# Output projection of a conv block: one PSUM bank a pair, the condition in PSUM for the shift columns, more low parts on Pool

## The chip, the cores and the metric

The kernel runs on one core of a Trainium2 chip. The metric is the device time of one execution in microseconds (us); lower is better. Three runs of the kernel before gave 1113.10, 1115.33 and 1116.34 us, a median of 1115.33.

Engines are named as in the profile: PE (TensorE, matrix products), DVE (VectorE), ACT (ScalarE), POOL (GpSimd) and SP (SyncE, which issues nearly all loads here). SBUF is the large on-chip memory and PSUM the small one into which PE writes. Here PSUM holds eight banks of 512 fp32 values for each of 128 partitions.

## What is computed

One decoder layer with a convolution mixer, on 256 tokens of width 2048, all in fp32. The part of the reference that runs:

```
cond = silu(c)
mod = cond @ mod_w + mod_b
sh1, sc1, g1, sh2, sc2, g2 = split(mod, 6)
h = rms_norm(x, norm1_g) * (1 + sc1) + sh1
u = h @ w_in + b_in;  a, gt = split(u, 2);  u = a * sigmoid(gt)
u = causal_depthwise_conv(u, dw_w, 31 taps) + dw_b
u = silu(layer_norm(u, ln_g, ln_b))
y = u @ w_out + b_out
x = x + (1 + g1) * y
h = rms_norm(x, norm2_g) * (1 + sc2) + sh2
x = x + (1 + g2) * (square(relu(h @ mlp_w1)) @ mlp_w2)
```

The change lies in `u @ w_out`, the residual behind it, and the computation of `sh2`, which runs in the same stage.

## The kernel before

**Splitting.** A matrix product in fp32 is made of three products of rounded parts. Each weight block `w` of 128 x 2048 values (one megabyte) is split in two halves of 128 x 1024: the high part `hi` is a rounding copy on ACT (line 203), and the low part `lo = w - hi` is a subtraction (line 206) on DVE or, for the jobs that the list `POOLED` (line 59) names, on POOL. There are six buffers for halves of each kind. The input is split likewise into tiles `hl` (lines 212 to 217, eight tiles of 256 columns of K). For the output product `mm` then issues, for each of 16 steps over K, three matmuls of 256 tokens: high x high (L227), high weight x low input (L228), low weight x high input (L229).

**Jobs.** `jobs` is a list of 16 input pairs, 8 output pairs and the MLP's blocks. A job `("out", i)` is pair i of 128-column tiles of the output projection, i from 0 to 7: two weight blocks, 96 matmuls. Ahead of each job the program splits the weights of the next one (`splits`). Pair 0 runs with K as its outer loop, since its input is still being normalised; pairs 1 to 7 do the first tile of the pair, then the second. Each pair accumulates in a tile `p` of the pool name "mm", of which there are two, each of two banks (line 779); the two tiles of the pair lie in different banks.

**Behind a pair** (lines 897 to 922): ACT scales and shifts both tiles in PSUM (L905), DVE adds the residual (L906), ACT squares (L908), POOL adds the squares up (L910, L913), ACT applies the second norm's scale (L917) and the result is split for the MLP (L214 on ACT, L217 on DVE).

**Shift columns.** `sh2` is a matrix-vector product done on DVE: 16 column blocks of 128 x 2048 of `mod_w`, one megabyte each, are multiplied with the condition, which is held broadcast to all partitions as `cb` in SBUF, and summed along the row in the same instruction (line 381, `mod_col`). `LATE_OUT` (line 51) places 1, 2, 2, 3, 3, 3, 1 and 1 of them behind pairs 0 to 7. At the end of pair 7 the bias is added (L928) and the shift is copied to a tile `shz` (L929), which the first job of the MLP multiplies (L322).

**Loads.** All blocks come through five buffers named "raw" in one order on SP (lines 163 to 184): the two blocks of the next pair, then the columns of this one. A load starts when one of the five is free: a weight block frees its buffer after its four split instructions, a column after its product.

**Order.** The order of instructions on each engine is fixed when the program is built, by a scheduler with priorities (`urgent`) and hand-made dependencies (`tc.issue_after`). Each engine runs its own instructions in order. PSUM tiles: "mm" two tiles of two banks, "acc" two tiles of one bank (`ps_two`, line 420), "small" and "row" one bank each. Ahead of the output stage "acc" holds the results of the SiLU that makes `hl` (lines 871 to 883).

Of the kernel before, what the change touches and what calls it, by code (L numbers as in the profile page):

```python
# [8 lines left out]
F32 = mybir.dt.float32  # L9
F32R = mybir.dt.float32r  # L10
AF = mybir.ActivationFunctionType
ALU = mybir.AluOpType
PSUM = bass.MemoryType.PSUM

P = 128
T = 256
D = 2048
KT = D // P
# [16 lines left out]
SH1, SC1, G1, SH2, SC2, G2 = range(6)  # L35
# [20 lines left out]
K_OUTER = [("out", 0), ("up", 0, 1)]  # L56
SIDE = 14
SPLIT_LOADS = [("col", SC1 * KT + KT - 1), ("col", SH1 * KT + KT - 1), ("first", KT - 1)]
POOLED = [("out", 0), ("out", 1), ("out", 2), ("up", 0, 1), ("up", 0, 2)]
LATE_GATE = {("down", 0): [1, 2, 1, 2, 2, 2, 1, 1], ("down", 1): [1, 1, 1, 1, 0, 0, 0, 0]}  # L60


# [1 line left out]
def conv_block(ctx: ExitStack, tc: tile.TileContext, x, vec, dwq, c_row, mod_r, mod_c, w_first, w_in, w_out, w1, w2, out):  # L64
    nc = tc.nc
# [15 lines left out]
    def col(name, j=0, n=1):  # L81
        at = VEC[name] + j
        return v[:, at : at + n]
# [79 lines left out]
    def top_up():  # L163
        while todo and waiting[home(todo[0])] < room[home(todo[0])]:
            key = todo.pop(0)
            tag = home(key)
            waiting[tag] += 1
            if tag == "raw":
                raw[key] = wts.tile([P, KT, P], F32, name="raw", bufs=RAW)
            elif tag == "first":  # L170
                raw[key] = start_pool.tile([P, 2 * HELD, P], F32, name="first", bufs=FIRST)
            elif tag == "x":
                raw[key] = x_pool.tile([P, KT, T], F32, name="x1")
            else:
                raw[key] = v[:, soon:]
                with tc.issue_after(state["load"].ins):
                    state["load"] = nc.sync.dma_start(dwq_sb, dwq)
            with tc.issue_after(state["load"].ins) if "load" in state else ExitStack():
                if key in SPLIT_LOADS:
                    first_half = nc.sync.dma_start(raw[key][:, 0:HALF], source(key)[:, 0:HALF])  # L180
                    with tc.issue_after(first_half.ins):
                        state["load"] = nc.sync.dma_start(raw[key][:, HALF:], source(key)[:, HALF:])
                else:
                    state["load"] = nc.sync.dma_start(raw[key], source(key))
# [27 lines left out]
    def split_act(dst, src, on_act=True):  # L212
        if on_act:
            state["hi_end"] = nc.scalar.activation(dst[:, :, 0:T], src, AF.Copy).ins  # L214
        else:
            nc.vector.tensor_copy(dst[:, :, 0:T], src)
        state["lo_end"] = nc.vector.tensor_tensor(dst[:, :, T : 2 * T], src, dst[:, :, 0:T].bitcast(F32), op=ALU.subtract).ins  # L217
# [158 lines left out]
    def mod_col(at):  # L376
        w = take(("col", at)).rearrange("p k n -> p (k n)")
        which, k = divmod(at, KT)
        acc = modc[:, at : at + 1]
        with tc.issue_after(state["e_end"]) if "e_end" in state else ExitStack():  # L380
            nc.vector.scalar_tensor_tensor(w, w, 1.0, cb, op0=ALU.mult, op1=ALU.mult, accum_out=acc)  # L381
        if which in amps:
            return nc.vector.scalar_tensor_tensor(
                amps[which][:, k : k + 1], acc, col("modb", at), col("n1g", k), op0=ALU.add, op1=ALU.mult
            )
        elif which != SH2:
            return mod_bias(at, 1, acc)

    def mods(keys):
        for key in keys:  # L390
            if key[0] == "mod":
                mod_chunk(*key[1:])
            else:
                mod_col(key[1])
# [25 lines left out]
    def ps_two():  # L420
        return ps.tile([P, 2, T], F32, name="acc", bufs=2)
# [40 lines left out]
    def by_tokens(job):  # L462
        return job[0] == "down" or job[0] == "up" and job[1:] not in ((0, 0), (0, 1))
# [300 lines left out]
    for n, job in enumerate(jobs):  # L764
# [10 lines left out]
            for key in parts_early:  # L775
                split_w(key, nc.gpsimd)
        kind, i = job[0], job[-1]
        if not by_tokens(job):
            p = ps.tile([P, 2, 2 * T], F32, name="mm", bufs=2)
        if by_tokens(job) and i % 2 == 0:  # L780
            sums[kind, i // 2] = regions(job == ("down", QUARTERS - 1, HALF - 2))
# [26 lines left out]
        if kind == "in":  # L808
# [46 lines left out]
            nc.gpsimd.memset(shz, 0.0)  # L855
            shc = x_pool.tile([P, 2 * UNSCALED], F32, name="shc")
            gb = x_pool.tile([P, KT], F32, name="gb")
            top_up()
            with tc.issue_after(state["sum_end"].ins):
                mods(rows[1:-1])  # L860
# [36 lines left out]
        if kind == "out":  # L897
# [21 lines left out]
                )  # L919
            xa[i] = mp.tile([P, 2, 2 * T], F32R, name="u2", bufs=HALF)  # L920
            split_act(xa[i], a)
            mods(after[job])
            if i == HALF - 2:
                table(AF.Abs_reciprocal_sqrt, ss[:, 0, 0:1])
            if i == HALF - 1:
                mod_finish()
                cs = slice(SH2 * KT, SH2 * KT + KT)
                nc.vector.tensor_tensor(modc[:, cs], modc[:, cs], col("modb", SH2 * KT, KT), op=ALU.add)  # L928
                nc.scalar.activation(shz[:, :, 0], modc[:, SH2 * KT : SH2 * KT + KT], AF.Copy)  # L929
                sp = ps.tile([P, 512], F32, name="small", bufs=1)  # L930
                column_sum(sp[:, 0:T], [sqacc, ss[:, 0, :], ss[:, 1, :]])
                r2 = sp[:, 0:T]
                rms_factor(sp[:, 0:T], sp[:, T : 2 * T], r2)
# [112 lines left out]
```

## Time and profile before

The profile is of one execution of 1112.88 us, whose span from the first instruction to the last is 1110.9 us, at a mean granted TensorE clock of 0.996.

| what | value |
|---|---|
| median of three runs | 1115.33 us |
| profiled execution | 1112.88 us |
| its span | 1110.9 us |
| output stage (first matmul of pair 0 to the shift row, L322) | 302.1 to 409.5 us |
| stage's column products, L381 on DVE, 16 | 41.8 us busy |
| stage's low parts on DVE, L206, up to 440 us | 28, 40.1 us busy |

A row of a time line gives the start in us from the span's start, the length, the engine, the line, the operation with output and inputs and their shapes, a count, and in brackets how long the engine had been idle and what ended that. A row of the view by line or tile gives the shortest, median and longest duration in ns. Durations of PE overlap, so its pace is read from the distance of the starts.

### The profile page before, as it was taken

The numbers are of one execution on the slowest core, as the hardware profiler recorded it, in microseconds if no ns is written. First come the engines' busy times: TensorE is split into PE (matmuls) and PEld (weight loads), VectorE is DVE, ScalarE is ACT, GpSimd is POOL, SyncE is SP. The second block draws the span as 40 slices with busy tenths as digits, with TensorE's granted clock in tenths as the row PEclk, the third lists the DMA queues.
The fourth block names the chain that finished last, engine by engine and source line by source line (L and its number), as shares of the span: only waits on it lengthen the run. The fifth ranks groups of instructions, "written<-read, shape, count | busy, mean of one in ns | idle before, by whom it ended". The sixth has DMA issues, their size and how long they took to land.

```text
span 1110.9 us, 15369 instructions
## 1 busy us (share of the span) xinstructions
PE 1087.3 (98%) x6018; PEld 893.0 (80%) x6018; DVE 767.9 (69%) x1014; ACT 506.7 (46%) x675; POOL 176.6 (16%) x106
## 2 busy tenths in 40 slices
PE   6999999999999899999999999999999999999998
PEld 3888876667699888888888888888888888888887
DVE  5777789987499987675885566744656565565553
ACT  4111396754674478443444444333444334444431
POOL 0000176467574244000000000000000000000000
PEclk8999999999999999999999999999999999999999
DMA  9999989878579976897997889857888967788641
GB/s 384 420 422 421 416 325 359 344 294 352 218 302 354 375 295 243 265 273 230 381 401 259 227 243 287 305 157 260 248 240 234 246 205 228 217 243 250 209 142 38
DMA packets 142314, 314.22 MB, mean 283 GB/s; under 512 B 87585, under 2 KB 105505, under 8 KB 107297
## 3 DMA queue, kind: packets, MB, share of 16 engines
q1 hardware_dynamic: 142096, 313.11, 81.3%
q8 instruction: 47, 0.77, 0.3%
q14 instruction: 25, 0.20, 0.1%
q10 hardware_dynamic: 146, 0.13, 0.0%
HBM read 301.15 MB, written 12.07 MB: 282 GB/s over the span
## 4 chain that ended last, share of the span: by engine, by line
PE 80%; DMA 10%; DVE 5%; issue 2%; POOL 2%; ACT 1%; SPq 0%; DVEq 0%; POOLq 0%; ACTq 0%
PE mm L255 20%; PE mm L254 20%; PE mm L256 20%; DMA raw<-mod_c 8%; PE mm L231 6%; PE mm L232 3%; DVE raw L381 3%; PE row L307 2%; PE mm L723 2%; DMA raw<-w_out 1%; POOL lo L206 1%; DVE lo L206 1%; PE mm L228 1%; PE mm L229 1%; PE mm L227 1%
## 5 line engine op out<-in xcount | busy, mean ns | idle before, releaser
L203 ACT ACTIVATE hi<-raw 128x1024 fp32r<-128x1024 f32 x320 | 334.2, 1058 | 355.6 <-PE mm L256 301.0
L206 DVE TENSOR_TENSOR lo<-raw,hi 128x1024 fp32r<-128x1024 f32 x269 | 332.7, 1246 | 173.0 <-ACT hi L203 172.5
L255 PE MATMUL mm<-lo,u 128*128 128x512 f32 x496 | 193.1, 389 | 0.0
L254 PE MATMUL mm<-hi,u 128*128 128x512 f32 x496 | 193.0, 389 | 0.0
L256 PE MATMUL mm<-hi,u 128*128 128x512 f32 x496 | 192.9, 389 | 0.0
L256 PE MATMUL mm<-hi,hl 128*128 128x512 f32 x480 | 186.7, 389 | 0.0
L255 PE MATMUL mm<-lo,hl 128*128 128x512 f32 x480 | 186.7, 389 | 0.0
L254 PE MATMUL mm<-hi,hl 128*128 128x512 f32 x480 | 186.7, 389 | 0.0
L381 DVE SCALAR_TENSOR_TENSOR raw<-raw,cond 128x2048 f32<-128x2048 f32 x62 | 147.1, 2374 | 47.6 <-DMA raw<-mod_c 47.5
L206 POOL TENSOR_TENSOR lo<-raw,hi 128x1024 fp32r<-128x1024 f32 x51 | 130.7, 2591 | 205.1 <-ACT hi L203 205.1
L255 PEld LDWEIGHTS mm<-lo,u 128*128 128x128 f32 x496 | 93.1, 188 | 19.4 <-DVE lo L206 0.4
L256 PEld LDWEIGHTS mm<-hi,u 128*128 128x128 f32 x496 | 93.1, 188 | 19.4
L254 PEld LDWEIGHTS mm<-hi,u 128*128 128x128 f32 x496 | 93.1, 188 | 19.0
L256 PEld LDWEIGHTS mm<-hi,hl 128*128 128x128 f32 x480 | 90.1, 188 | 18.8
L254 PEld LDWEIGHTS mm<-hi,hl 128*128 128x128 f32 x480 | 90.1, 188 | 18.8
L255 PEld LDWEIGHTS mm<-lo,hl 128*128 128x128 f32 x480 | 90.1, 188 | 18.6
L615 DVE SCALAR_TENSOR_TENSOR acc<-u,v,acc 128x256 f32<-128x256 f32 x224 | 94.5, 488 | 1.9
L229 PE MATMUL mm<-hl,lo 128*128 128x256 f32 x288 | 81.8, 284 | 3.4 <-DVE lo L206 3.2
L227 PE MATMUL mm<-hl,hi 128*128 128x256 f32 x288 | 81.2, 284 | 3.6 <-ACT hi L203 2.2
L231 PE MATMUL mm<-hl,hi 128*128 128x512 f32 x224 | 81.9, 406 | 0.0
L228 PE MATMUL mm<-hl,hi 128*128 128x256 f32 x288 | 81.6, 284 | 0.2 <-DVE hl L217 0.2
L550 PE MATMUL mm<-two,first 128*128 128x256 f32 x256 | 60.6, 391 | 8.4 <-ACT two L581 8.4
(170 smaller groups left out, 1189.6 us busy)
## 6 DMA issues: line engine op xcount, KB each, us to landing
raw<-w SPq DMA_DIRECT2D x128, 1024.0 KB, 5.4
raw<-mod_c SPq DMA_DIRECT2D x62, 1024.0 KB, 9.2
raw<-mod_r SPq DMA_DIRECT2D x32, 1024.0 KB, 7.7
raw<-w_in SPq DMA_DIRECT2D x16, 1024.0 KB, 7.0
raw<-w_out SPq DMA_DIRECT2D x16, 1024.0 KB, 7.0
first<-w_first SPq DMA_DIRECT2D x15, 1024.0 KB, 17.1
flat<-two SPq DMA_DIRECT2D x30, 256.0 KB, 2.7
two<-flat SPq DMA_DIRECT2D x120, 64.0 KB, 4.2
```

The lines of the kernel that those rows point to most:

```text
L203: state["w_hi"] = nc.scalar.activation(hi, w[:, ks, :], AF.Copy).ins
L206: end = by.tensor_tensor(lo, w[:, ks, :], hi.bitcast(F32), op=ALU.subtract)
L227: nc.tensor.matmul(out_p, w, m[:, 0:T], start=begin, stop=False)
L228: nc.tensor.matmul(out_p, w, m[:, T : 2 * T], start=False, stop=False)
L229: state["mm_end"] = nc.tensor.matmul(out_p, lo[:, k % HALF, :], m[:, 0:T], start=False, stop=end)
L231: nc.tensor.matmul(p[:, c, :], hi[:, k % HALF, :], m, start=(k == 0), stop=(k == KT - 1))
L254: nc.tensor.matmul(p, p_hi, hi, start=begin, stop=False)
L255: nc.tensor.matmul(p, p_hi, lo, start=False, stop=False)
L256: nc.tensor.matmul(p, p_lo, hi, start=False, stop=end)
L381: nc.vector.scalar_tensor_tensor(w, w, 1.0, cb, op0=ALU.mult, op1=ALU.mult, accum_out=acc)
L550: step = nc.tensor.matmul(held[n][:, c, :], w[:, 2 * n + c, :], h, start=k == 0 and c == 0, stop=k == KT - 1, skip_group_check=True)
L615: nc.vector.scalar_tensor_tensor(out, s, w, acc, op0=ALU.mult, op1=ALU.add)
```

## The change

It does four things in the output stage.

- Pairs 1 to 7 accumulate both tiles in one bank, a tile of the "acc" pool; pair 0 keeps "mm".
- Behind pair 1 the condition is copied by ACT into both "mm" tiles, 1024 values in each. The column products behind pairs 1 to 5 (13 of the 16) are done as two instructions of 1024 values, with the condition read from PSUM and the two sums in `modc` and a new tile `rest2`; the hand-made dependency on `e_end` is left out there. Behind pair 6 the copies are given up, and the last two columns are done as before, as is the one behind pair 0.
- The low parts of pairs 3, 4 and 5 move from DVE to POOL (`POOLED`), 12 halves.
- The bias is added to `rest2`, and `rest2` to the shift, where one addition stood.

```
-POOLED = [("out", 0), ("out", 1), ("out", 2), ("up", 0, 1), ("up", 0, 2)]
+POOLED = [("out", i) for i in range(6)] + [("up", 0, 1), ("up", 0, 2)]
+IN_PSUM = range(1, 6)
...
         acc = modc[:, at : at + 1]
+        if which == SH2 and "cond" in state:
+            n = HALF * P
+            for half, total in zip(state["cond"], (acc, rest2[:, k : k + 1])):
+                nc.vector.scalar_tensor_tensor(w[:, 0:n], w[:, 0:n], 1.0, half, op0=ALU.mult, op1=ALU.mult, accum_out=total)
+                w = w[:, n:]
+            return
         with tc.issue_after(state["e_end"]) if "e_end" in state else ExitStack():
...
-        if not by_tokens(job):
+        if kind == "out" and i > 0:
+            p = ps_two()
+        elif not by_tokens(job):
             p = ps.tile([P, 2, 2 * T], F32, name="mm", bufs=2)
...
+            rest2 = x_pool.tile([P, KT], F32, name="rest2")
+            nc.gpsimd.memset(rest2, 0.0)
...
             split_act(xa[i], a)
+            if i == IN_PSUM[0]:
+                state["cond"] = []
+                for h in range(2):
+                    half = ps.tile([P, 2, 2 * T], F32, name="mm", bufs=2).rearrange("p a b -> p (a b)")
+                    nc.scalar.activation(half, cb[:, h * HALF * P : (h + 1) * HALF * P], AF.Copy)
+                    state["cond"].append(half)
+            if i == IN_PSUM[-1] + 1:
+                del state["cond"]
             mods(after[job])
...
-                nc.vector.tensor_tensor(modc[:, cs], modc[:, cs], col("modb", SH2 * KT, KT), op=ALU.add)
+                nc.vector.tensor_tensor(rest2, rest2, col("modb", SH2 * KT, KT), op=ALU.add)
+                nc.vector.tensor_tensor(modc[:, cs], modc[:, cs], rest2, op=ALU.add)
```

SP issues the same loads in the same order. On POOL the twelve new low parts stand between the sums of squares.

## The prediction

> **What bounds the kernel now.** I read the page first, then the busy time of the engines in four stretches of the output stage, then TensorE's own rows around each wait, and last the rows of the engines that it waits for.
>
> ```profile
> span 1110.9 us, 15369 instructions
> ...
> PE 1087.3 (98%) x6018; PEld 893.0 (80%) x6018; DVE 767.9 (69%) x1014; ACT 506.7 (46%) x675; POOL 176.6 (16%) x106
> ```
>
> PE is busy 98% of the span, so a change elsewhere is worth only what PE now loses in waits. The edit touches one stage, pairs 0 to 7 of the output product, which the windows show (after each engine's time, the instructions; then clock, DMA share, GB/s):
>
> ```profile
> core 0: us, PE busy (x) PEld busy (x) DVE busy (x) ACT busy (x) POOL busy (x), PEclk, DMA share, GB/s
> 302.00:326.80 24.80, 24.44 (x200) 24.06 (x201) 22.19 (x31) 18.79 (x31) 17.54 (x8) 1.00 0.86 346
> 326.80:361.90 35.10, 34.97 (x292) 34.76 (x291) 35.10 (x28) 18.67 (x28) 20.08 (x10) 1.00 0.87 329
> 361.90:402.80 40.90, 35.50 (x290) 34.69 (x289) 37.78 (x35) 24.15 (x35) 7.61 (x7) 1.00 0.95 364
> ```
>
> The stretches are pairs 0 and 1, 2 to 4, and 5 to 7. DVE is full from pair 2 on, POOL has room, and in pairs 5 to 7 PE is idle for some 5 us. PE's rows name each wait (start, length, and in brackets the idle time before it and what ended that):
>
> ```profile
> 335.69 0.28 PE L228 MATMUL mm<-hl,hi 128*128 128x256 f32 x1
> 336.11 0.39 PE L229 MATMUL mm<-hl,lo 128*128 128x256 f32 x1
> ...
> 361.89 0.28 PE L227 MATMUL mm<-hl,hi 128*128 128x256 f32 x1
> 362.01 0.28 PE L228 MATMUL mm<-hl,hi 128*128 128x256 f32 x1
> 363.06 0.39 PE L229 MATMUL mm<-hl,lo 128*128 128x256 f32 x1 [0.78 <-DVE lo L206]
> ...
> 374.43 0.28 PE L227 MATMUL mm<-hl,hi 128*128 128x256 f32 x1
> 374.55 0.28 PE L228 MATMUL mm<-hl,hi 128*128 128x256 f32 x1
> 376.52 0.39 PE L229 MATMUL mm<-hl,lo 128*128 128x256 f32 x1 [1.69 <-DVE lo L206]
> ...
> 387.78 0.28 PE L229 MATMUL mm<-hl,lo 128*128 128x256 f32 x1
> 390.23 0.38 PE L227 MATMUL mm<-hl,hi 128*128 128x256 f32 x1 [2.17 <-ACT hi L203]
> ...
> 391.49 0.38 PE L229 MATMUL mm<-hl,lo 128*128 128x256 f32 x1 [0.76 <-DVE lo L206]
> ...
> 409.48 0.75 PE L322 MATMUL row<-raw,shz 128*32 128x128 f32 x20
> ```
>
> Products start 0.12 us apart (361.89, 362.01), so a step's excess over 0.12 is the loss: 0.30 in pair 2, 0.93 in pair 5, 1.85 in pair 6, and 2.33 and 0.92 in pair 7: 6.3 us. Pair 5 lasts from 361.89 to 374.43, 12.54 us; without its wait a pair is 11.6, or 96 products at 0.121. Counting back from 361.89 over three pairs and 0.30, pair 1 ends at 326.8; forward from 390.23 by 11.6 and 0.92, pair 7 ends at 402.8.
>
> **Why the low parts are late.** DVE and POOL hold each other up:
>
> ```profile
> 314.23 21.82 POOL L206 TENSOR_TENSOR lo<-raw,hi 128x1024 fp32r<-128x1024 f32 x6 [7.26 <-ACT hi L203]
> 314.54 4.24 DVE L381 SCALAR_TENSOR_TENSOR raw<-raw,cond 128x2048 f32<-128x2048 f32 x1
> 323.14 0.68 DVE L906 TENSOR_TENSOR x<-mm,x 128x512 f32<-128x512 f32 x1
> ...
> L381 DVE SCALAR_TENSOR_TENSOR raw<-raw,cond x62: 2277/2290/4239, 13.0 to 703.7; 128x2048 f32<-128x2048 f32 x62
> L206 POOL TENSOR_TENSOR lo<-raw,hi x51: 2375/2407/4480, 134.5 to 430.3; 128x1024 fp32r<-128x1024 f32 x51
> L206 DVE TENSOR_TENSOR lo<-raw,hi x269: 1181/1224/3424, 133.5 to 1091.4; 128x1024 fp32r<-128x1024 f32 x135
> L367 DVE SCALAR_TENSOR_TENSOR raw<-raw,cond x4: 1218/1224/1227, 123.5 to 127.9; 128x1024 f32<-128x1024 f32 x4
> ```
>
> A column product takes 2.29 us at the median and 4.24 where POOL holds a low part; POOL's takes 2.41 at the median and 4.48 at most, 3.64 on average in the run of six. Each excess (1.95 and 2.07) is about the other's length less its head start, so one waits until the other is through. L906, with one operand in PSUM, keeps its 0.68 us inside the same run of POOL. The eight products of L876, likewise half in PSUM, do so too:
>
> ```profile
> 296.80 10.17 POOL L875 TENSOR_TENSOR two<-cv,mu 128x512 f32<-128x512 f32 x8 [2.59 <-ACT mu L867]
> 299.53 1.88 DVE L876 TENSOR_TENSOR two<-two,small 128x512 f32<-128x512 f32 x3
> ```
>
> They stand 0.6 us apart while POOL goes on at 1.27. The Trainium skill ("SBUF — State Buffer", Who interferes with whom) states the same as a rule: two inputs in SBUF go through a read port shared with GpSimd and exclude it, one input doesn't. By that rule the new column products would not exclude POOL, and the trace agrees for L906 and L876 (0.68 us beside POOL).
>
> No row here shows the very form that is new, a product with a running sum and one operand in PSUM; that it excludes POOL all the same is rival B.
>
> **The change, part by part.**
>
> 1. *Twelve low parts of pairs 3 to 5 leave DVE.* That is 12 x 1.22 = 14.6 us, from an engine that is full from pair 2 to the start of pair 7. They cost POOL 12 x 2.41 = 29 us.
>
> 2. *Thirteen columns in halves, the condition in PSUM.* Nearest row: 1.22 us for a 1024-wide half in SBUF, 2.45 a column against 2.29, so 13 x 0.16 = 2.1 us more on DVE. From below it is nothing more than L381's rate (2.29); from above, 0.07 us more a half if PSUM costs what it seems to in L615 (0.488 us for 256 elements, where L413 takes 0.426):
>
> ```profile
> L615 DVE SCALAR_TENSOR_TENSOR acc<-u,v,acc 128x256 f32<-128x256 f32 x224 | 94.5, 488 | 1.9
> L413 DVE SCALAR_TENSOR_TENSOR small<-small,two 128x256 f32<-128x256 f32 x2 | 0.9, 426 | 1.0 <-ACT two L409 1.0
> ```
>
> I take 1.22. DVE is relieved of over 12 us on balance, which covers either end.
>
> 3. *Does POOL hold the pace?* Its six first low parts begin at 314.2 as before. The column of pair 0 is still a plain one and blocks the second, so the third starts at 321.1; the other columns no longer block, and four parts at 2.35 end at 330.5 instead of 336.0. PE needs the last of them in pair 2 at about 337, so the 0.30 goes. The first sum of squares makes it 331.4. Then, up to the last part of pair 5, stand 12 low parts (28.2), five sums (4.5 at 0.9) and four blocks by the residual's low part L217 (2.8): 366.9. The first part of pair 5 is ready about four parts or sums earlier, at 359, and PE wants it at 363.6 (pair 1's end in part 5, and three pairs of 11.6). POOL has 4.6 us in hand: the 0.93 goes.
>
> 4. *Pair 6* keeps its low parts on DVE, which now has nothing to finish first but a column each: the 1.85 goes. *Pair 7* still waits. Its high parts stand on ACT behind the eviction of pair 6:
>
> ```profile
> 388.10 1.11 ACT L905 ACTIVATE mm<-mm,gb,modc 128x256 f32<-128x256 f32 x2 [7.70 <-PE mm L229]
> 389.13 1.99 ACT L203 ACTIVATE hi<-raw 128x1024 fp32r<-128x1024 f32 x2
> ```
>
> In the built order one eviction instead of two stands ahead of them, so about 0.55 of 2.33 goes, and the 0.92 for the low part stays: 2.7 of 3.25 are left.
>
> 5. *One bank a pair from the "acc" pool.* This is what is lost. Before, pair 1's sums lie in "mm", and the built order puts 33 of its products among pair 0's, where PE would otherwise wait for the normalised input (hl). Now pair 1 needs an "acc" bank, which that stage's own results hold until the end, and only 11 products of pair 1 stand ahead of pair 0's last, all after its 84th. So PE follows the input:
>
> ```profile
> 311.25 1.29 DVE L217 TENSOR_TENSOR hl<-acc,hl 128x512 fp32r<-128x512 f32 x2
> 313.93 0.69 DVE L217 TENSOR_TENSOR hl<-acc,hl 128x512 fp32r<-128x512 f32 x1
> 315.07 0.95 PE L354 MATMUL row<-v,rowsb 128*128 128x4 f32 x8
> ```
>
> Input pair 5's low part is ready at 311.95. Eleven more products bring 313.3, one more and the row fold (0.95) 314.4, 34 products the end of pair 0 at 318.5 (the last input, ready at 314.6, is in time), 85 more the end of pair 1: 328.8 instead of 326.8. Loss 2.0. The same in the other direction: no loss if PE were never behind the input, which 33 borrowed products contradict.
>
> 6. *Two copies of the condition on ACT*, about 1.05 us each as the high parts (two in 1.99 above). The second waits for pair 0's eviction and lies beside PE's pair 1. The first stands early in the input's chain. ACT waits there twice for DVE, 0.36 and 0.58:
>
> ```profile
> 305.24 2.37 ACT L880 ACTIVATE acc<-two,v 128x256 f32<-128x256 f32 x4 [0.36 <-DVE hl L217]
> 308.83 2.16 ACT L880 ACTIVATE acc<-two,v 128x256 f32<-128x256 f32 x4 [0.58 <-DVE hl L217]
> ```
>
> That hides 0.94 of 1.05. I take 0.1; the bounds are 0 and 1.05. Columns of pair 1 keep their weight buffers until the second copy, near 330 instead of 323 and 328, but the low parts free theirs sooner, so loads aren't later. SP's order does not change.
>
> 7. *The end of the stage.* From pair 7's end PE needs 6.7 us to L322, 0.2 of it waiting for the shift columns, which end sooner: 0.2 goes. Two sums for one at the end are 16 elements wide: nothing.
>
> **Sum.** +2.0 + 0.1 - 0.30 - 0.93 - 1.85 - 0.55 - 0.2 = -1.7 us. Behind the stage PE's rows show no wait that would swallow it. The profiled execution has a span of 1110.9 in a time of 1112.88 and goes to 1111.2. The median of the runs is 1115.33, 2.45 above it: 1113.6 us, 0.15% less. 0.3%, or 3.35 us, is about what a measurement of this kernel can tell from no change.
>
> **Rivals.**
>
> *B, slower: the halves exclude POOL after all.* Place: POOL's queue for pairs 3 to 5. Then the low parts and columns stand in one line: from 321.1, 16 parts (37.6), sums (5.4), ten columns (23.0) and four L217 (2.8) end at 390 instead of 367, where PE wants the last part at 372.3 (the fourth of four quarters of pair 5): 17 us late. Less the margin that the estimate may overstate, some 15 over the forecast: 1128. It decides once POOL is blocked over 4.6 us before pair 5, 0.3 us for each of the 16 halves of pairs 2 to 4's eight columns. For it: two SBUF operands do this in row L381, and POOL then has no room. Against it: L906 and L876.
>
> *C, faster: pair 7's wait goes too.* If its high parts slipped ahead of the eviction, 2.7 more would go: 1110.9. For it: ACT is idle 7.7 us just there. Against it: the engine is in order, and the built order keeps the eviction first.
>
> *D, the loads keep the pace down.* Pairs 3 to 5 each need two weight blocks and three columns, 5.24 MB in 11.6 us, or 452 GB/s; the stretch ran at 364 with the DMA engines 95% busy. If that holds pairs 5 and 6 back as now, only 0.30, 0.55 and 0.2 go against 2.1, or 3.0 with the copy unhidden: +1.0 to +2.0, 1117. Against it: buffers came free late then, because DVE was behind, and pairs 6 and 7 need just three blocks each.
>
> **How the numbers follow.** Forecast 0.50, B 0.13, C 0.21, D 0.16. The forecast alone spans 1111 (copy free, 1 us less lost at the start) to 1116 (copy unhidden, PSUM dearer, a wait in pair 6). Range 1109.5 to 1118.5: below, C and the 1.5 us that the shown runs stray; above, D with the same; it leaves out B and a few in a hundred. Faster by over 0.3% (below 1112.0): nearly all of C and a quarter of the forecast, 0.32. Slower (above 1118.7): B and a little of D, 0.16. Between: 0.52.
>
> **What would show it.** Right: the halves near 1.2 us while POOL's low parts stay at 2.4; no wait at L229 in pairs 2, 5 and 6; some 2 us of PE idle before pair 1; 1.8 us before pair 7. Wrong: halves of 2 us or more, or POOL parts of 3.5 (B); PE without a hole at the start; waits for DMA on w_out (D).

## The result, and the profile after

The changed kernel takes 1111.49 us (median; 1109.66 to 1113.64) against 1114.29 us (1113.06 to 1116.34) for the kernel before on the same chip: a ratio of 0.9975, 95% interval 0.9964 to 0.9985, or 1.7 to 4.0 us less. The prediction had 1113.6 us within 1109.5 to 1118.5, and "within 0.3%" as the likeliest outcome. Its direction and range hold. The median itself lies 2.1 us below the forecast, about half of it because the forecast started from 1115.33, the median of three runs, and half because the kernel gained more; against that start 1111.49 would even lie below the 1112.0 that was set down as the bound of a gain of over 0.3%. What the prediction made of the edits one by one holds only in part, as the runs below show.

Lines of the changed kernel are one higher than before at L203 to L322: L204 makes the high parts, L207 the low parts, L228 to L230 are the three products, L384 is the new column product of half width, L388 the plain one, L916 the eviction (L905 before). First the page, with the busy time of each engine:

```profile
span 1110.4 us, 15401 instructions
...
PE 1089.3 (98%) x6018; PEld 894.6 (81%) x6018; DVE 745.8 (67%) x1029; ACT 506.9 (46%) x677; POOL 191.7 (17%) x119
```

22 us have left DVE and 15 have come to POOL. The windows over the same three stretches as before (PE, PEld, DVE, ACT, POOL busy, with instructions; granted clock, DMA share, GB/s):

```profile
302.00:326.80 24.80, 23.34 (x186) 22.53 (x187) 18.79 (x32) 18.20 (x30) 17.30 (x9) 1.00 0.82 323
326.80:361.90 35.10, 35.10 (x295) 35.10 (x294) 22.65 (x32) 22.16 (x33) 32.90 (x18) 1.00 0.97 376
361.90:402.80 40.90, 38.54 (x304) 38.04 (x303) 36.04 (x46) 22.81 (x34) 11.07 (x10) 0.96 0.88 343
```

In pairs 2 to 4 DVE has 12 us of room, POOL only 2, and PE isn't idle at all. In the first stretch PE works 1.1 us less than before, though its stage began 0.56 us earlier here (first product at 301.58, not 302.14). In the third the granted clock is 0.96, where it was 1.00 before; that matters below. PE's own rows, at the start of each pair and around the waits:

```profile
301.58 0.38 PE L228 MATMUL mm<-hl,hi 128*128 128x256 f32 x1 [1.40 <-ACT hl L215]
302.31 0.39 PE L229 MATMUL mm<-hl,hi 128*128 128x256 f32 x1 [0.34 <-DVE hl L218]
...
304.20 0.38 PE L228 MATMUL mm<-hl,hi 128*128 128x256 f32 x1 [0.32 <-DVE hl L217]
305.39 0.39 PE L229 MATMUL mm<-hl,hi 128*128 128x256 f32 x1 [0.81 <-DVE hl L218]
...
328.38 0.28 PE L228 MATMUL acc<-hl,hi 128*128 128x256 f32 x1
...
363.18 0.28 PE L230 MATMUL acc<-hl,lo 128*128 128x256 f32 x1
...
374.70 0.28 PE L230 MATMUL acc<-hl,lo 128*128 128x256 f32 x1
...
387.74 0.38 PE L228 MATMUL acc<-hl,hi 128*128 128x256 f32 x1 [1.60 <-ACT hi L204]
387.96 0.28 PE L229 MATMUL acc<-hl,hi 128*128 128x256 f32 x1
389.00 0.38 PE L230 MATMUL acc<-hl,lo 128*128 128x256 f32 x1 [0.76 <-DVE lo L207]
```

328.38 is the first product of pair 2; 363.18 and 374.70 are the third products of pairs 5 and 6, where 0.78 and 1.69 us of idle time stood before. Of the old waits only the two before pair 7 are left, and new ones stand at the start. Last, the groups of column products and low parts in the stage (302 to 402.8; busy time, mean ns of one):

```profile
L207 POOL TENSOR_TENSOR lo<-raw,hi 128x1024 fp32r<-128x1024 f32 x18 | 45.0, 2529 | 9.7 <-ACT hi L204 9.7
L384 DVE SCALAR_TENSOR_TENSOR raw<-raw,mm 128x1024 f32<-128x1024 f32 x26 | 30.7, 1215 | 10.1 <-DMA raw<-mod_c 7.3 <-ACT mm L937 2.4 <-issue 0.2
L207 DVE TENSOR_TENSOR lo<-raw,hi 128x1024 fp32r<-128x1024 f32 x12 | 14.6, 1263 | 4.5 <-ACT hi L204 4.4
L388 DVE SCALAR_TENSOR_TENSOR raw<-raw,cond 128x2048 f32<-128x2048 f32 x3 | 9.3, 3117 | 0.0
```

The halves take 1.215 us beside POOL's low parts at 2.53 on average. The three plain columns that are left take 3.1 on average; the one that meets a low part on POOL takes 4.25.

**A ruler for all the runs.** The stage has 768 products, 96 to a pair, all in the trace. Counted in PE's rows, the distance from the first product's start to that of the 193rd (pair 2), the 577th (pair 6) and the 673rd (pair 7) places every loss, whatever the stage's own start. In the kernel before it is 24.74, 72.29 and 88.09 us; in the changed one 26.80, 72.88 and 86.15. A pair without waits takes 11.52.

### The profile page after: what moved, and what is told of

It reads as the page before. It is cut to its first block, busy times and chain, and to the rows that moved or that the text cites. A ratio compares the mean times of both kernels' runs of the same rounds, so it can differ in the third digit from the quotient of the medians.

```text
span 1110.4 us, 15401 instructions
## 1 busy us (share of the span) xinstructions
PE 1089.3 (98%) x6018; PEld 894.6 (81%) x6018; DVE 745.8 (67%) x1029; ACT 506.9 (46%) x677; POOL 191.7 (17%) x119
## 4 chain that ended last, share of the span: by engine, by line
PE 82%; DMA 11%; DVE 4%; SPq 1%; ACT 1%; issue 0%; DVEq 0%; ACTq 0%
PE mm L256 18%; PE mm L257 18%; PE mm L255 18%; DMA raw<-mod_c 9%; PE mm L232 6%; PE mm L233 3%; DVE raw L388 3%; PE acc L230 2%; PE acc L228 2%; PE acc L229 2%; PE row L308 2%; PE mm L730 2%; DMA flat<-two 1%; PE mm L229 1%; SPq L275 1%; DVE lo L207 1%
## 5 line engine op out<-in xcount | busy, mean ns | idle before, releaser
L204 ACT ACTIVATE hi<-raw 128x1024 fp32r<-128x1024 f32 x320 | 333.7, 1056 | 359.7 <-PE mm L257 292.8
L207 DVE TENSOR_TENSOR lo<-raw,hi 128x1024 fp32r<-128x1024 f32 x257 | 311.7, 1222 | 168.4 <-ACT hi L204 168.1
L207 POOL TENSOR_TENSOR lo<-raw,hi 128x1024 fp32r<-128x1024 f32 x63 | 152.3, 2445 | 206.3 <-DMA raw<-w_in 132.3
L388 DVE SCALAR_TENSOR_TENSOR raw<-raw,cond 128x2048 f32<-128x2048 f32 x49 | 114.5, 2339 | 51.9 <-DMA raw<-mod_c 51.9
L228 PE MATMUL acc<-hl,hi 128*128 128x256 f32 x224 | 64.2, 287 | 1.6 <-ACT hi L204 1.6
L230 PE MATMUL acc<-hl,lo 128*128 128x256 f32 x224 | 64.2, 287 | 0.8 <-DVE lo L207 0.8
L557 PEld LDWEIGHTS mm<-two,first 128*128 128x128 f32 x256 | 50.0, 197 | 17.5 <-ACT two L588 10.5
```

The lines of the kernel that those rows point to most:

```text
L204: state["w_hi"] = nc.scalar.activation(hi, w[:, ks, :], AF.Copy).ins
L207: end = by.tensor_tensor(lo, w[:, ks, :], hi.bitcast(F32), op=ALU.subtract)
L228: nc.tensor.matmul(out_p, w, m[:, 0:T], start=begin, stop=False)
L230: state["mm_end"] = nc.tensor.matmul(out_p, lo[:, k % HALF, :], m[:, 0:T], start=False, stop=end)
L557: step = nc.tensor.matmul(held[n][:, c, :], w[:, 2 * n + c, :], h, start=k == 0 and c == 0, stop=k == KT - 1, skip_group_check=True)
```

## What the prediction left open: which edit does what

The sum came out right, but it ascribed to each edit what the trace of before shows as a wait. The runs take the edits apart, and the last two profile both kernels again. In the table all times are in us, the ratio is to the kernel before on the same chip, and the last three columns are the distances of the ruler in each kernel's profiled execution.

| kernel | median | ratio, 95% | pair 2 | pair 6 | pair 7 |
|---|---|---|---|---|---|
| before | 1114.29 | | 24.74 | 72.29 | 88.09 |
| changed | 1111.49 | 0.9975 (0.9964 to 0.9985) | 26.80 | 72.88 | 86.15 |
| 1 columns plain again | 1123.53 | 1.0092 (1.0077 to 1.0108) | 26.54 | 84.00 | 99.14 |
| 2 low parts back on DVE | 1109.68 | 0.9964 (0.9952 to 0.9977) | 26.80 | 72.88 | 86.16 |
| 3 before, banks alone | 1112.61 | 0.9988 (0.9979 to 0.9997) | 26.55 | 72.89 | 87.41 |
| 4 copies later | 1110.84 | 0.9970 (0.9959 to 0.9982) | 26.54 | 72.62 | 85.90 |
| 5 pair 1 in mm | 1111.12 | 0.9979 (0.9971 to 0.9988) | 24.74 | 72.13 | 86.16 |
| 6 eviction after high part | 1107.50 | 0.9947 (0.9935 to 0.9960) | 28.24 | 74.31 | 85.83 |
| 7 = 5 and 6 | 1108.12 | 0.9952 (0.9939 to 0.9964) | 25.99 | 72.12 | 84.07 |
| 8 = 7, low parts on DVE | 1107.52 | 0.9948 (0.9934 to 0.9961) | 24.74 | 71.23 | 83.69 |
| 9 before, eviction alone | 1110.39 | 0.9967 (0.9955 to 0.9980) | 26.00 | 72.26 | 85.73 |
| 10 = 6, low parts on DVE | 1107.33 | 0.9939 (0.9925 to 0.9952) | 28.44 | 74.52 | 86.04 |

(In 6, 7, 9 and 10 a dip of the granted clock in pair 0 of the profiled execution holds 1.25 to 1.64 us of the distance to pair 2. Kernels 2 and 4 have a dip there too, but their pair 2 comes no later than without one: 26.80 as in the changed kernel, and 26.54 as in kernel 1. The dips are dealt with at the end.)

### 1. The columns plain again

```diff
-            if i == IN_PSUM[0]:
-                state["cond"] = []
-                for h in range(2):
...
-            if i == IN_PSUM[-1] + 1:
-                del state["cond"]
```

> The changed kernel, with its column products of pairs 1 to 5 plain again: 2048 wide, both operands in SBUF; the low parts of six pairs stay on POOL and the sums keep their bank each. Theory (what the change lives on is that products with the condition in PSUM do not exclude POOL): columns again near 4.2 us where POOL holds a low part, POOL's low parts near 4.4 us where a column holds it, and POOL's queue, which now has no room, ends pair 5's last low part some 15 us late: 1111.5 + 12 to 16, about 1125. Rival (POOL's and DVE's excesses in the kernel before are a matter of loads and order, not of operands): columns 2.3, low parts 2.4, and the time within 2 us of the changed kernel's 1111.5.

Measured: 1123.53 us, 12 us over the changed kernel's median. Its groups in the same stretch, and two of PE's waits:

```profile
L207 POOL TENSOR_TENSOR lo<-raw,hi 128x1024 fp32r<-128x1024 f32 x18 | 62.5, 3496 | 7.2 <-ACT hi L204 7.2
L388 DVE SCALAR_TENSOR_TENSOR raw<-raw,cond 128x2048 f32<-128x2048 f32 x14 | 50.4, 3611 | 5.6 <-DMA raw<-mod_c 3.3 <-POOL lo L207 2.3
```

```profile
355.46 0.39 PE L230 MATMUL acc<-hl,lo 128*128 128x256 f32 x1 [2.36 <-POOL lo L207]
...
378.23 0.39 PE L230 MATMUL acc<-hl,lo 128*128 128x256 f32 x1 [1.86 <-POOL lo L207]
```

The same 18 low parts cost POOL 62.5 us instead of 45.0, a column 3.6 instead of two halves at 1.2, and PE now waits for POOL. This is rival B's price, which the prediction put at 15 us; it is paid when the operand is in SBUF and not when it is in PSUM. Behind the two waits shown the granted clock also falls to half for 3.41 us each, so waiting isn't all of the 12 us. The edit changes the width of the products too, but width alone doesn't explain it: DVE's low parts in the kernel before, 1024 wide with both operands in SBUF, are held up as well (3.42 us for the first two of pair 3).

### 2. The low parts of pairs 3 to 5 back on DVE

```diff
-POOLED = [("out", i) for i in range(6)] + [("up", 0, 1), ("up", 0, 2)]
+POOLED = [("out", i) for i in range(3)] + [("up", 0, 1), ("up", 0, 2)]
```

> The changed kernel, with the low parts of pairs 3 to 5 back on DVE (condition in PSUM, a bank a pair). Theory (moving the low parts is what takes the waits of pairs 5 and 6 away, and freeing POOL from the columns alone does half of it): DVE was busy 36.7 of the 49.7 us from 326.8 to 376.5 in the changed kernel; twelve low parts at 1.22 add 14.6 and make 51.3, so DVE is full again and 1 to 1.6 us of wait come back in pairs 5 and 6: 1112.5 to 1113. Rival (the products in PSUM alone took the waits, since blocked columns and low parts cost DVE about 11 us in the kernel before: columns 2.64 and low parts 1.53 on average): no wait in pairs 5 and 6 and the changed kernel's time, 1111.5. Second rival (the low parts are all of it): the 2.8 us of pairs 5 and 6 come back whole, 1114.3.

Measured: 1109.68 us, not slower than the changed kernel, and pair 7 at 86.16 against 86.15. Pairs 2 to 4 and DVE's groups:

```profile
326.80:361.90 35.10, 35.10 (x295) 35.10 (x294) 33.99 (x44) 21.80 (x32) 10.13 (x9) 1.00 0.99 397
```

```profile
L384 DVE SCALAR_TENSOR_TENSOR raw<-raw,mm 128x1024 f32<-128x1024 f32 x26 | 30.5, 1212 | 5.1 <-DMA raw<-mod_c 2.7 <-ACT mm L937 2.4
L207 DVE TENSOR_TENSOR lo<-raw,hi 128x1024 fp32r<-128x1024 f32 x24 | 30.3, 1306 | 5.0 <-ACT hi L204 5.0
```

DVE is almost full again (33.99 of 35.10) and PE still never waits. My expectation, a wait of 1 to 1.6 us, was wrong, and the first rival right: moving these twelve low parts buys nothing. What DVE lacked before was not their 14.6 us. The same grouping of the kernel before:

```profile
L381 DVE SCALAR_TENSOR_TENSOR raw<-raw,cond 128x2048 f32<-128x2048 f32 x15 | 39.5, 2640 | 0.4 <-DMA raw<-mod_c 0.4
L206 DVE TENSOR_TENSOR lo<-raw,hi 128x1024 fp32r<-128x1024 f32 x23 | 34.1, 1526 | 2.7 <-ACT hi L203 2.7
```

Against 2.29 and 1.22 us undisturbed, that is 15 x 0.35 + 23 x 0.30 = 12 us that DVE lost to POOL. In experiment 2 some 4.5 of them are left (24 low parts at 1.306, three plain columns at 3.1), so the condition in PSUM removes most of the loss. The banks are changed here too, but by themselves, in experiment 3, they leave DVE's low parts at 1.44 us on average.

### 3. The banks alone, on the kernel before

```diff
-        if not by_tokens(job):
+        if kind == "out" and i > 0:
+            p = ps_two()
+        elif not by_tokens(job):
```

> The kernel before, with only the sums of pairs 1 to 7 moved to a bank each of the pool acc. Theory 1 (the loss at the start of the stage adds to all else, as the prediction's sum has it): pair 1 ends 1.7 to 2.0 us later, the waits of pairs 2, 5, 6 and 7 stay: 1114.3 + 1.7 to 2.0 = 1116.0 to 1116.3. Theory 2 (DVE's queue, not TensorE, sets when the low parts are ready, so a TensorE that is late at the start only waits less later): pair 1 ends as late, but the waits of pairs 2, 5 and 6 shrink by up to the same 1.7, and the time is 1114.3 to 1114.6.

Measured: a ratio of 0.9988, 0.3 to 2.3 us less than before rather than more. In PE's rows pair 2 begins late, and then:

```profile
328.41 0.28 PE L227 MATMUL acc<-hl,hi 128*128 128x256 f32 x1
```

```profile
376.14 0.39 PE L229 MATMUL acc<-hl,lo 128*128 128x256 f32 x1 [0.98 <-DVE lo L206]
```

```profile
389.28 0.38 PE L227 MATMUL acc<-hl,hi 128*128 128x256 f32 x1 [1.60 <-ACT hi L203]
```

328.41 is 1.81 us later after the stage's first product than before. By pair 6 only 0.60 of it is left (72.89 against 72.29): pair 5 has no wait at all, pair 2 lost 0.45 and loses 0.26. Pair 6 then waits 0.98 instead of 1.69, and the step to pair 7 has 1.60 of idle time instead of 2.17, since one eviction and not two stands ahead of the high part. Theory 2 holds, and the loss goes further than it said: the low parts come when DVE has them, so a PE that arrives later waits less.

### 4. The copies behind the last SiLU

```diff
-                    nc.scalar.activation(half, cb[:, h * HALF * P : (h + 1) * HALF * P], AF.Copy)
+                    with tc.issue_after(state["silu"]):
+                        nc.scalar.activation(half, cb[:, h * HALF * P : (h + 1) * HALF * P], AF.Copy)
```

> The changed kernel, with the two copies of the condition put on ScalarE behind the last SiLU of the normalised input. Theory (the copy lies inside ScalarE's waits for DVE in that chain, the prediction's 0.1 us): within 0.3 us of 1111.5, and pair 1 ends within 0.3 us of where it did. Rival (the copy's 1.02 us is late in full, since input pair 1's low part came 3.76 us after the start of the stage and before 3.06): 0.7 to 1.0 us less, 1110.5 to 1110.8, unless POOL, which then has its first unblocked columns later, gives it back.

Measured: pair 2 at 26.54 instead of 26.80, and pair 7 0.25 earlier. The copy's share is 0.26 us (experiment 3, which has no copies, gives 26.55 as well): more than the 0.1 I took, inside its bounds of 0 and 1.05. The two ratios can't be told apart (0.9970 and 0.9975).

### 5. Pair 1 back in mm

```diff
-IN_PSUM = range(1, 6)
+IN_PSUM = range(2, 6)
...
-        if kind == "out" and i > 0:
+        if kind == "out" and i > 1:
```

> The changed kernel, with pair 1's sums in mm again and its two columns plain, so that the condition is copied and the columns halved from pair 2 on. Theory (the loss of 1.65 us before pair 1 ends, read from the trace of the changed kernel, is the lost loan of pair 1's products, and POOL has time in hand): the three waits of 0.3 to 0.8 us at the start go, one of up to 0.3 us comes at pair 2 as in the kernel before, no other; pair 7 begins 1.3 to 1.65 us earlier after the stage's first product than the changed kernel's 86.16 us, and the time is 1109.8 to 1110.2. Rival (as in the kernel before, what TensorE gains at the start it waits for later, since two more plain columns block POOL for 2 us each and low parts come later): waits at pairs 2 to 5 that eat the 1.65, 1111.5.

Measured: 0.9979, the same as the changed kernel. The loan of pair 1's products is back, and pair 2 begins 24.74 us after the first product, as before. Then:

```profile
326.16 0.28 PE L228 MATMUL acc<-hl,hi 128*128 128x256 f32 x1
```

```profile
362.17 0.39 PE L230 MATMUL acc<-hl,lo 128*128 128x256 f32 x1 [1.04 <-POOL lo L207]
```

```profile
387.59 0.39 PE L228 MATMUL acc<-hl,hi 128*128 128x256 f32 x1 [2.17 <-ACT hi L204]
```

All of the 2.06 us gained at the start is given back: pair 5 takes 1.30 more, because POOL, blocked by two more plain columns (its low parts take 2827 ns here, 2529 in the changed kernel), is late with its low part; and from pair 6 to pair 7 it is 0.76 more, 0.57 of it since two evictions stand ahead of the high part again. Pair 7 begins at 86.16 against 86.15. The rival holds: here POOL, not PE, sets the pace up to pair 5, and ScalarE's order sets it at pair 7.

### 6. Pair 6's eviction behind pair 7's first high part

```diff
                 state["w_hi"] = nc.scalar.activation(hi, w[:, ks, :], AF.Copy).ins
+            if key == ("out", HALF - 1, 0):
+                state["hi_7"] = state["w_hi"]
...
-                    nc.scalar.activation(t2[:, c, :], t2[:, c, :], AF.Identity, scale=mcol(G1, k), bias=gb[:, k : k + 1])
+                    with tc.issue_after(state["hi_7"]) if i == HALF - 2 else ExitStack():
+                        nc.scalar.activation(t2[:, c, :], t2[:, c, :], AF.Identity, scale=mcol(G1, k), bias=gb[:, k : k + 1])
```

> The changed kernel, with pair 6's eviction put on ScalarE behind pair 7's first high part. Theory (the 1.76 us before pair 7 are the eviction ahead of the high part in ScalarE's queue, and its block of weights has landed by 382.05, 4 us before the eviction begins): the high and low part are made ahead of pair 6's end, both waits go, 1.76 + 0.92 = 2.7 us less: pair 7 begins 84.4 us after the stage's first product instead of 86.16 and has no second wait, 1108.8. Rival 1 (the high part alone gains, the low part stays late): 1.76 less, 1109.7. Rival 2 (the wait is for the load, not for the queue): 1111.5.

Measured: 1107.50 us, 0.9947: some 3 us below the changed kernel. ScalarE's rows, then DVE's (L209 makes the low parts here, L919 is the eviction):

```profile
381.05 2.01 ACT L204 ACTIVATE hi<-raw 128x1024 fp32r<-128x1024 f32 x2 [1.09 <-DMA raw<-w_out]
387.51 1.11 ACT L919 ACTIVATE acc<-acc,gb,modc 128x256 f32<-128x256 f32 x2 [4.46 <-PE acc L232]
```

```profile
383.18 2.36 DVE L209 TENSOR_TENSOR lo<-raw,hi 128x1024 fp32r<-128x1024 f32 x2
```

The high part begins as soon as its weights have landed and is done 4.4 us before the eviction can start; the low part follows. In PE's rows no wait is left behind pair 0: pairs 6 and 7 follow each other without a gap (85.83 - 74.31 = 11.52). Theory and size hold: both waits go, 1.76 and 0.92 us.

### 7 and 8. Both of the last two, and the low parts on DVE

> The changed kernel with the edits of the last two together: pair 1 in mm, and pair 6's eviction behind pair 7's first high part. If both losses are what they seem and don't hang together: 1.3 to 1.65 and 2.7 us less, 1107.1 to 1107.5. If TensorE, so much earlier, waits for POOL's low parts of pairs 2 to 5 or for pair 7's block of weights instead: 1108.5 or more, with those waits in TensorE's rows.

> The last kernel, with the low parts of pairs 3 to 5 on DVE. Theory (where products in PSUM leave POOL alone, it doesn't matter which of the two engines makes these low parts, as long as neither is full): the last kernel's time within 0.5 us. Rival (DVE was busy 33.99 of the 35.10 us of pairs 2 to 4 with these low parts; two blocked columns of pair 1 at 4.2 us for four halves at 1.22 ask 3.5 more, so DVE is 2.4 us short): a wait of 1 to 2.4 us in pairs 4 to 6, and that much over the last kernel.

Measured: 0.9952 and 0.9948, no better than 6. In 7, PE is early and waits for pair 7's weights instead (PE's rows, then ScalarE's):

```profile
385.69 0.39 PE L230 MATMUL acc<-hl,hi 128*128 128x256 f32 x1 [0.28 <-ACT hi L204]
385.91 0.28 PE L231 MATMUL acc<-hl,hi 128*128 128x256 f32 x1
387.28 0.39 PE L232 MATMUL acc<-hl,lo 128*128 128x256 f32 x1 [1.10 <-DVE lo L209]
```

```profile
384.57 2.01 ACT L204 ACTIVATE hi<-raw 128x1024 fp32r<-128x1024 f32 x2 [5.62 <-DMA raw<-w_out]
```

The block landed some 3.5 us later than in 6 (384.57 against 381.05, where in both the high part starts at the landing). Most of that delay arises before the transfer: SP issued the load at 374.53, and at 371.81 in 6. In 8 DVE is full (34.77 of the 35.10 us of pairs 2 to 4) and PE waits for its low parts in pairs 6 and 7:

```profile
373.70 0.39 PE L232 MATMUL acc<-hl,lo 128*128 128x256 f32 x1 [0.69 <-DVE lo L209]
```

```profile
386.52 0.38 PE L232 MATMUL acc<-hl,lo 128*128 128x256 f32 x1 [1.05 <-DVE lo L209]
```

The second outcome set down for 7 holds for its waits, though not as far as 1108.5. For 8 the theory holds in the time (0.6 us less, within the runs' spread) and the rival in the waits. Whoever makes pair 1 earlier finds the next limit at once: POOL (experiment 5), DVE (8) or the load (7).

### 9. The eviction alone, on the kernel before

The edit of experiment 6, and nothing else.

> The kernel before, with nothing but pair 6's eviction put on ScalarE behind pair 7's first high part. Theory (that wait is one of the queue's order, and the change isn't needed to remove it): pair 7's first block of weights landed at 384.20 in the kernel before, so the high part can be done by 386.3, 3.9 us before it is wanted, and the 2.33 us go; its low part stands on DVE behind columns that end at 388.7 and is made by 389.95, so that about 1.7 us of wait come back at pair 7's third product instead of 0.92: 1.5 us less than the kernel before, ratio 0.9986. If DVE makes the low part ahead of its columns, both waits go, 3.25 us, ratio 0.997. Rival (pair 7 waits for its load in this kernel): no gain.

Measured: 0.9967 (0.9955 to 0.9980), as good as the whole change. PE's row, and what DVE did until then:

```profile
389.38 0.39 PE L231 MATMUL mm<-hl,lo 128*128 128x256 f32 x1 [1.69 <-DVE lo L208]
```

```profile
385.90 2.28 DVE L383 SCALAR_TENSOR_TENSOR raw<-raw,cond 128x2048 f32<-128x2048 f32 x1
...
388.12 2.35 DVE L208 TENSOR_TENSOR lo<-raw,hi 128x1024 fp32r<-128x1024 f32 x2
```

As expected, the low part stands behind the column that ends at 388.2, and PE waits there. In the trace the stage up to the first product that works on its result is 1.52 us shorter (99.44 against 100.96), the 1.5 of the theory. The runs show 2.2 to 5.0 us less. The rest isn't in the waits; the clock (below) is the likeliest cause, and these runs don't prove it.

### 10. The eviction, and the low parts on DVE

> The changed kernel, with pair 6's eviction behind pair 7's first high part and the low parts of pairs 3 to 5 back on DVE: what the runs so far leave of the change as its working parts, with the order of the eviction. Theory: the same as the run with the eviction alone, which took 0.9947 of the kernel before: 1107 to 1108, and no wait of TensorE after pair 0. Rival (DVE, full with these low parts, is late with pair 7's): a wait of up to 1 us at pairs 6 or 7 and 0.5 to 1 us more.

Measured: 1107.33 us, 0.9939 (0.9925 to 0.9952): no wait of PE behind pair 0, the theory's outcome. This is the lowest of all, 6.8 us below the kernel before, though 6, 7 and 8 lie within its interval.

### 11 and 12. Both kernels profiled again

> The kernel before, unchanged, profiled a second time. If its waits are the program's own: the step before pair 7 and those of pairs 2, 5 and 6 within 0.1 us of the first profile, 88.09 us from the stage's first product to pair 7's, 12.5 us for pair 7. The stage's first product, at 302.14 in its first profile and at 301.4 to 301.9 in all others: near 301.5 if that was the one execution, at 302.1 if it is the kernel's own.

> The changed kernel, unchanged, profiled a second time. If the 14.0 us of its pair 7 are a dip of the granted clock in that one execution: here 12.5 us, where the clock stays at 1.00 from 388 to 396, or again 14.0 where it does not. If they are the change's own (a wait that the rows don't show): 14.0 with the clock at 1.00. In either case 86.15 us from the stage's first product to pair 7's, within 0.1 us, unless the clock dips before.

Measured: 1115.73 us for the kernel before, 1111.13 for the changed one, one execution each. The waits are the program's own: 88.07 and 86.16 us to pair 7. The first product came at 301.64 in the kernel before, so the 302.14 of its first profile was that one execution's. But pair 7, 12.51 us from its first product to its last in the first profile of the kernel before, took 15.15 in the second, and 14.01 and 14.00 in the two of the changed kernel. Three sets of windows (after the length, the first number is PE's busy time; the third from the right is the granted clock). They are 3.41 us long and are set where the clock of that execution changes: the kernel before, first and second profile, and the changed kernel, first profile.

```profile
386.17:389.58 3.41, 1.89 (x16) 1.69 (x15) 2.97 (x5) 1.45 (x3) 0.00 (x0) 1.00 0.99 389
389.58:392.99 3.41, 2.00 (x14) 1.80 (x15) 2.71 (x3) 3.39 (x6) 1.20 (x1) 1.00 0.96 389
```

```profile
386.76:390.17 3.41, 1.24 (x9) 0.88 (x7) 2.70 (x4) 2.56 (x4) 0.00 (x0) 1.00 0.94 384
390.17:393.59 3.42, 2.66 (x13) 2.62 (x13) 1.88 (x2) 3.39 (x7) 2.11 (x2) 0.50 1.02 388
393.59:397.00 3.41, 3.41 (x18) 3.41 (x18) 2.59 (x3) 3.41 (x5) 0.00 (x0) 0.50 0.92 267
```

```profile
386.50:389.91 3.41, 1.41 (x9) 1.21 (x10) 2.19 (x2) 3.41 (x5) 0.00 (x0) 1.00 0.83 344
389.91:393.33 3.42, 3.42 (x18) 3.42 (x17) 3.42 (x4) 3.40 (x6) 1.61 (x2) 0.50 0.71 228
```

The longer pair 7 comes with a dip of the clock in both kernels; the second profile of the changed kernel has the same one, 3.41 us at half clock from 389.29. Experiment 2's profile, where pair 7 begins at the same 86.16 and the clock stays at 1.00 there, has 12.51 again. So the dip, not the change, makes the 14.0, and experiment 2 has the changed kernel's stage as it is by itself: 105.27 us from the first product to the row sum of L323, against 107.34 to L322 in the first profile of the kernel before.

## Why the prediction was right, point by point

**The start (+2.0 for the banks, +0.1 for the copy).** Measured 26.80 - 24.74 = 2.06: 1.81 from the banks (experiment 3) and 0.25 from the copy. Both terms are off, by 0.19 and 0.15 in opposite directions, so that their sum is right to 0.04 by luck.

**The waits of pairs 2, 5 and 6 (-0.30, -0.93, -1.85) and the shorter step to pair 7 (-0.55).** All go, each a little larger than forecast: pair 2 is 0.45 shorter, pair 5 1.02, and pair 6 with the step to pair 7 2.53, where 1.85 and 0.55 make 2.40. But experiment 3 shows that pair 5's wait and part of pair 2's go already because PE comes later, by the very loss that the sum adds at the start.

**Pair 7's second wait, and the end (-0.2).** 0.76 us of idle time stands at L230 as it did. Behind pair 7's start the stage is 0.14 shorter (88.09 to 107.34, and 86.16 to 105.27 in experiment 2).

**The sum.** -1.94 and -0.14 make -2.08, where the prediction had -1.73. The median fell by 2.8 us, with an interval from 1.7 to 4.0 that holds both. None of the prediction's terms is a dip of the clock, and profiles of both kernels hold some, so how near the two numbers come is in part chance.

**The halves and POOL.** Halves of 1.215 us against 1.22; POOL's low parts at 2529 ns on average over 18, one of them held by pair 0's plain column. That one apart, the queue of part 3 came out to the point: its last part of pair 5 ends at 366.9. The 0.07 us more a half, set down as an upper bound, came from a comparison that doesn't show it: the rows of L615 and L413 both read one operand from PSUM. The halves took no longer than the 1.22 us of L367 with both in SBUF. The rival of exclusion falls, and experiment 1 shows its price to be real. The Trainium skill ("SBUF — State Buffer", Who interferes with whom) states that a VectorE instruction with at most one input in SBUF, outside the two-port modes, doesn't contend with GpSimd. The groups of the changed kernel and of experiment 1 agree, for this form too (1.215 and 3.6 us).

**What was wrong: part 1 of the change.** "Twelve low parts of pairs 3 to 5 leave DVE" was set down as the relief that takes the waits of pairs 5 and 6. Experiment 2 keeps them on DVE and loses nothing. The relief was the blocking, which the prediction had read from the rows of L381 and L206 but priced only for POOL's queue, in part 3, and not for DVE's.

**What was right by its company: part 5.** The start's loss counts in full only because the change takes the later waits away as well. By itself it costs nothing (experiment 3), and undoing it, with pair 1's two columns plain again, gains nothing (experiment 5). The sum holds since it compared two whole timelines; its terms aren't prices of the edits.

**Rival C.** ScalarE's order does hold pair 7 back, as the prediction said, and an edit of three lines reverses it: 2.7 us forecast and some 3 measured (experiment 6). **Rival D** (loads) didn't come: the DMA engines moved 376 GB/s in pairs 2 to 4, where 329 was the rate before. In experiment 7 PE does come to wait for a block of weights, chiefly because its load starts later.

**The offset.** The prediction added 2.45 us between the profiled execution and the median as a constant of the kernel. The second profile of before, 2.85 us longer than the first, has 2.64 of them in pair 7's dip of the clock. So the offset was at least in part a cost that hangs on the very wait before pair 7. That the first profile of before had no such dip was luck: its wait fell on two windows of the clock and not on one.

## What to carry to other kernels

Where DVE and POOL both read two operands from SBUF, count what each loses to the other before moving work between them: here one operand in PSUM gave DVE the room that moving twelve instructions was meant to give. A wait read from a trace is the difference of two arrivals, so price an edit by asking what else arrives late at the same product; a loss upstream of a wait may cost nothing, and a gain there may buy nothing. And look first at what stands ahead in an in-order queue: three lines that let a ready high part pass an eviction were worth as much as the whole change.

## What the runs showed of the hardware

After a wait, the clock granted to TensorE can fall to half, and the traces show when. Its changes lie on a grid: in all fourteen traces the times between two changes are multiples of 3.41 us, but the grid lies elsewhere in each execution. Cut the output stage of every trace along its own grid. Each of the eleven windows at full clock in which PE was idle for 1.73 us or more was followed by one at half clock. Of the six with 1.62 to 1.70 us two were, and of those with 1.60 or less none. In a window at half clock, 0.61 to 0.76 us of idle time kept the clock at half for one more (three of three); with 0.50 or less it came back.

What counts is how much idle time falls into one window. The 2.17 us before pair 7 fell into one in the second profile of the kernel before, and the clock stayed at half for two windows, at a cost of 2.64 us in pair 7. In the first profile 1.52 us of idle time fell into one window and 1.41 into the next, and there was no dip. In the two profiles of the changed kernel 2.00 and 2.36 us fell into one, at a cost of 1.5 us each time. Idle times add up: in experiment 6 the 1.40 us ahead of the stage's first product and the 0.34 behind it make 1.74.

```profile
299.55:302.97 3.42, 1.68 (x15) 0.95 (x8) 2.72 (x6) 3.35 (x7) 3.42 (x4) 1.00 1.06 446
302.97:306.38 3.41, 2.80 (x13) 2.42 (x12) 3.40 (x7) 3.08 (x7) 3.33 (x3) 0.50 0.95 406
306.38:309.79 3.41, 3.41 (x18) 3.41 (x18) 2.56 (x5) 2.99 (x7) 0.00 (x0) 0.50 1.03 437
```

Pair 2 comes 1.44 us later there than in the changed kernel. So a wait of some 2 us costs TensorE its length and, in the executions in which it falls into one window of the grid, about as much again.

The Trainium skill ("TensorE: Matmul & The Clock Gate", What's actually happening) states a gate that goes to half rate after at least one idle window of about 3.4 us, in windows that run freely, so that it varies from run to run. The size, the half rate and the variation agree with these rows. The threshold doesn't: at most 2.36 of the 3.41 us of a window in this stage were idle (in experiment 1 and in the second profile of the changed kernel), and the clock fell all the same; the measurement decides.
